# The even mixer of a two-layer trunk: v projected ahead of q and k, recurrence outputs ahead of attention outputs, slices of a quarter

## The chip, the cores and the metric

The kernel runs on one core of one Trainium2 chip. The metric is the device time of one execution in microseconds (us); less is better. PE is the engine of the matrix multiplications, DVE, ACT and POOL are the vector, scalar and GpSimd engines, and SP issues the loads of the weights.

## What is computed

A trunk of two layers runs over 256 rows of 1024 values. Each layer is a feed-forward block (FFN), a mixer, and another FFN; the mixer of layer 0 is "even", that of layer 1 is "odd" (retention). Only the even mixer matters here. It runs differential attention and a recurrence (RWKV-7) side by side behind one input projection and joins them in one output projection:

```python
def diff_rwkv_mixer(h, w_in, w_out, ...):
    z = h @ w_in
    za, zb = z[..., :A_COLS], z[..., A_COLS:]        # attention | recurrence
    qa, ka, va = jnp.split(za, 3, axis=-1)
    ...
    oa = diff_attention(qa, ka, va, lam)             # softmax 0 - lam * softmax 1, per head
    oa = rms_norm(oa, subln) * (1.0 - lam_init)
    ob, v_b = rwkv7_time_mix(zb, mu, vec, w_up, a_up, g_up, v_first, vres)
    mix = jnp.concatenate([oa, ob], axis=-1)
    return mix @ w_out, v_b

def rwkv7_time_mix(zb, ...):
    zs = token_shift(zb, mu)                         # z + (previous row - z) * mu
    r, k, v, xw, xa, xg = jnp.split(zs, B_SPLITS, axis=-1)
    ...
    y = rwkv7_recurrence(rh, heads(decay), kh, vh, kk, heads(a))
    y = head_group_norm(y, ln_w, ln_b)
    y = y + bonus                                    # sum(r*k*r_k) * v, per head
    return y * g, v
```

## The kernel before

The 256 rows are two blocks of 128 (b = 0 and 1). Every product is made of three multiplications of split operands: a weight chunk of 128x1024 lands as `raw`, ACT rounds it into `wh` (L307), DVE subtracts to get the rest `wl` (L308), and PE multiplies the high and low halves of the activations with them. These casts and splits run through the whole kernel, and each `wh` waits for a buffer that PE has finished reading.

The even mixer is one generator per block, `even(b, ...)`, and the loop `run` interleaves the two by the table `turns`, which is made from `EVEN_ORDER`. It is a list of seven pieces of the input projection: k, r and "low" (the low-rank inputs) and v feed the recurrence; q2, k2 and v2 feed the attention. The pieces are the stream: long runs of multiplications whose operands are there early. Between them go jobs with long chains over several engines: `feature` (shifted k and r, through a transposition on PE), `low_rank`, then `rwkv_features` (which ends in the multiplications `pn` that need `kk` from ACT and `fr` from POOL), `rwkv` (the core: doubling steps L1175 to L1183 that invert small triangular matrices, then the grams `pk`, the outputs `py` and the norm), and `attention`. A piece of the stream stops at a `yield "slice", 1.4` in `proj_slices` or `features_slices`, and there the loop may put in one step of a job; the numbers beside each `yield` are estimates of how long a step takes on PE and when its results are there. `spawn` gives each job a rank, and the lowest rank that is due goes first. `room` keeps a step back until one of two PSUM buffers for such steps should be free. PE then runs in exactly this order (`manual_schedule`); the other engines follow an order that the scheduler makes from it.

Inside a block the order is: k, r, low, q2, k2, v, v2. Block 0 projects q and k for both blocks. `value` (the recurrence's v) scales z on ACT, moves it down one row by a DMA on POOL's queue (`zs<-z`, and for block 1 the last row of block 0, `ups`), and mixes on DVE in three operations (L840 to L842). It takes its buffers from `t2`, a ring of five that also holds the `z`, `zm`, `kk`, `low`, `mu`, `lnw` and `lnb` of the other jobs. After v2 come the output projections: each of the four rows of weights takes one transposed input, `att0`, `att1` from the attention and `mr0`, `mr1` from the recurrence, which `turn` makes with two PE transpositions (L387), ACT (L391, L394) and DVE (L392, L395). Then `post` normalises and adds to x, and the next FFN begins with transpositions of x (L434).

The output of the recurrence is a chain on DVE: copy of `py` (ACT L1303), mean (L1313), subtraction (L1315), square (ACT L1316), variance (L1318), a power on POOL (L406), scaling (L1320 to L1322), and the gate (L1325).

Of the kernel before, what the change touches and what calls it, by code (L numbers as in the profile page):

```python
# [41 lines left out]
U_FFN, U_EVEN, U_ODD = 3 * NCH, 17, 32  # L42


EVEN_ORDER = ("k", "r", "low", "q2", "k2", "v", "v2")
PLAN = [("ffn", 0, 0), ("even", 0, 0), ("ffn", 0, 1), ("ffn", 1, 0), ("odd", 1, 0), ("ffn", 1, 1)]
SIZES = {"ffn": U_FFN, "even": U_EVEN, "odd": U_ODD}

# [57 lines left out]
def _layout(inputs):  # L106
    a = {n: np.asarray(v) for n, v in inputs.items()}
    f = np.float32

    def cols(w, k_tiles=4):  # L110

        k, n = w.shape
        return w.reshape(-1, k_tiles, P, n).transpose(0, 2, 1, 3).reshape(-1, P, k_tiles * n)

    def ffn(l, j, i):
        c0, c1 = JOINT.get(i, JOINT[None])
        w = a["ffn_wgu"][l, j]

        solo = w.reshape(2, 4, P, 2, NCH, 256).transpose(4, 0, 2, 1, 3, 5).reshape(NCH, 2, P, 2048)
        both = w.reshape(8, P, 2, NCH, 256).transpose(3, 2, 1, 0, 4).reshape(NCH, 2, P, 2048)  # L120
        gu = np.concatenate([solo[:c0], both[c0:c1], solo[c1:]])
        dn = cols(a["ffn_wd"][l, j], 2)
        out = []
        for c in range(NCH):
            out += [gu[c, 0], gu[c, 1]]
            if c:
                out.append(dn[c - 1])
        return out + [dn[NCH - 1]]

    def even():  # L130
        w, out = a["even_w_in"][0], []
        b0 = 1536
        at = {"k": b0 + 512, "r": b0, "v": b0 + 1024, "q2": 0, "k2": 512, "v2": 1024}
        for c in EVEN_ORDER:
            if c == "low":
                out += list(cols(w[:, b0 + 1536 :], 8))
            elif c in ("q2", "k2"):
                out += [cols(w[:, i : i + 256], 8)[0] for i in (at[c], at[c] + 256)]
            else:
                out += list(cols(w[:, at[c] : at[c] + 512]))  # L140
        return out + list(cols(a["even_w_out"][0], 2))

    def odd():
        w, out = a["odd_w_in"][0], []
        wo = list(cols(a["odd_w_out"][0], 2))

        def ch(c):
            return list(cols(w[:, c : c + 512]))

        def head(c):  # L150
            return list(cols(w[:, c : c + 256], 8))

        for h in range(4):
            out += ch(2048 + h * 512) + ch(4096 + h * 512)
            if h:
                out += wo[2 * h - 2 : 2 * h]
            else:
                for c in range(0, 1024, 512):
                    out += head(c) + head(c + 256) + head(c + 1024) + head(c + 1280)
        return out + wo[6:8]  # L160

    units = []
    for i, (kind, l, j) in enumerate(PLAN):
        units += ffn(l, j, i) if kind == "ffn" else even() if kind == "even" else odd()
    wts = np.ascontiguousarray(np.stack(units))

    par = np.zeros((P, PR_N), f)

    def put(name, v):
        s, e = PR[name]  # L170
        par[: v.shape[0], s:e] = v

    nm = a["norms"]
    put("gpre", nm[:, 0::2].reshape(6, 8, P).transpose(2, 0, 1).reshape(P, 48))
    mu = a["rwkv_mu"][0]
    put("mu_r", mu[0:512].reshape(4, P).T)
    put("mu_k", mu[512:1024].reshape(4, P).T)
    s, _ = PR["mu_s"]
    par[:64, s] = mu[1536:1600]
    par[:64, s + 1] = mu[1600:1664]  # L180
    par[:, s + 2] = mu[1664:1792]
    w0, a0, k_k, k_a, r_k, ln_w, ln_b = a["rwkv_vec"][0]
    put("k_k", k_k.reshape(4, P).T)
    put("k_a", k_a.reshape(4, P).T)
    s, _ = PR["r_k"]
    for t in range(4):
        for h in range(2):
            par[h * 64 : h * 64 + 64, s + 2 * t + h] = r_k[t * P + h * 64 : t * P + h * 64 + 64]
    put("sub", a["diff_subln"][0][:, None])
    rows = np.concatenate([nm[:, 1::2].reshape(-1), mu[1024:1536], ln_w, ln_b, a["diff_lam"][0].reshape(-1)])  # L190
    ups = np.zeros((P, 3, 512), f)
    ups[:64, 0] = a["rwkv_w_up"][0]
    ups[64, 0] = w0
    ups[:64, 1] = a["rwkv_a_up"][0]
    ups[64, 1] = a0
    ups[:, 2] = a["rwkv_g_up"][0]
    c0, ce, co = _constants()
    return {
        "x": np.ascontiguousarray(a["x"].reshape(SEQ, D)),
        "wts": wts,  # L200
        "rows": np.ascontiguousarray(rows),
        "ups": ups,
        "c0": np.concatenate([c0, par], 1),
        "ce": ce,
        "co": co,
    }
# [6 lines left out]
class Trunk:  # L213
# [103 lines left out]
    def proj_slices(self, ps, u, first, last, xT, width=512):  # L317
        w = self.split[u]
        xh, xl = xT
        n = 2048 // width  # L320
        k0 = 0 if first else 8 - n
        mm = self.nc.tensor.matmul
        for i in range(n):
            h, l = w[2 * i // n]
            c = slice(i % (n // 2) * width, (i % (n // 2) + 1) * width)
            kt = k0 + i
            mm(ps[:, :width], lhsT=xh[:, kt, :], rhs=h[:, c], start=first and i == 0, stop=False)  # L327
            mm(ps[:, :width], lhsT=xh[:, kt, :], rhs=l[:, c], start=False, stop=False)  # L328
            mm(ps[:, :width], lhsT=xl[:, kt, :], rhs=h[:, c], start=False, stop=last and i == n - 1)  # L329
            if i == n // 2 - 1:  # L330
                yield "slice", 1.4

    def outp(self, acc, u, hT, first, last):
        w = self.split[u]
# [10 lines left out]
    def features_slices(self, ps, u):  # L345

        w, xh, xl = self.split[u], self.xh, self.xl
        mm = self.nc.tensor.matmul
        for t in range(2):
            o = ps[:, t * 256 : t * 256 + 256]  # L350
            for kt in range(8):
                h, l = w[kt // 4]
                c = slice(kt % 4 * 256 + t * P, kt % 4 * 256 + t * P + P)
                mm(o, lhsT=h[:, c], rhs=xh[:, kt], start=kt == 0, stop=False)
                mm(o, lhsT=h[:, c], rhs=xl[:, kt], start=False, stop=False)
                mm(o, lhsT=l[:, c], rhs=xh[:, kt], start=False, stop=kt == 7)
                if kt == 3 or (kt == 7 and not t):
                    yield "slice", 1.4

    def proj_parts(self, u, t):  # L360

# [340 lines left out]
    def even(self, b, u, l, j):  # L702
# [57 lines left out]
        def feature(ps, name, mu, om_at):  # L760
            z = scaled(ps, T2("z"))
            yield 0, 1.3
            yield from self.room(2.6)
            tp = transposes(z, 4)

            d = mx.tile([P, 4, P], F32, tag=f"av{'kr'.index(name)}" if b else f"f{name}", name=f"f{name}")
# [105 lines left out]
        for c in EVEN_ORDER:  # L872
            if c in ("q2", "k2"):
                for i in range(2):
                    if b == 0:
                        ps = self.ps("mm")
                        yield from self.features_slices(ps, u)
                        (queries if c == "q2" else keys)(i, ps)
                        self.stream_took = 1.4
                    else:  # L880
                        self.stream_took = 0
                    u += 1
                    if i and c == "k2":
                        att = self.spawn(1 + 3 * b, self.attention(b, S[f"qT{b}"], kT, rs), 1.5)
                    yield
                continue
            ps = self.ps("mm")
            if c != "low":
                yield from self.proj_slices(ps, u, True, False, xT)
                self.stream_took = 1.4  # L890
                u += 1
                if rs is None:
                    rs = self.rstd(b)
# [3 lines left out]
                    self.spread(b, rs)  # L897
            else:
                yield from self.proj_slices(ps, u, True, True, xT, 256)
            self.stream_took = 1.4  # L900
            u += 1
            if c in jobs:
                job = self.spawn(2 * b, jobs[c](ps))
                if c == "low":
                    core = S[f"core{b}"] = job
            else:
                with self.tc.high_priority(LIFT):
                    (value if c == "v" else values)(ps)
# [6 lines left out]
            return S["core0"]["done"] if b else "through1" in S  # L915

        acc = None
        for i, job in enumerate((att, att, core, core)):
            while not job["done"] or self.now < job["at"] or (acc is None and not free()):
                yield "wait"  # L920
            if acc is None:
                acc = [self.ps(("mm", "ac1")[b]) for _ in range(2)]
            self.outp(acc, u, S.pop(f"{'mr' if i > 1 else 'att'}{b}{i % 2}"), i == 0, i == 3)
            self.stream_took = 2.8
            u += 1
            if i == 3:
# [48 lines left out]
    def attention(self, b, qT, kT, rs):  # L975
# [5 lines left out]
        nsl = CE["nsl"][0]  # L981
        ss = self.small(4, "ss4", 2)
        ma = self.hx(b).bitcast(F32).rearrange("p (a t) -> p a t", a=4)
        for h0 in range(0, 4, H):
            heads = range(h0, h0 + H)

# [27 lines left out]
            for i in range(H):  # L1014
# [2 lines left out]
                    out=s[:, 0, i], in0=s[:, 0, i], scalar=ri[:, 0, i : i + 1], in1=s[:, 1, i],  # L1017
                    op0=ALU.mult, op1=ALU.add,
                )
            yield 1.7, 8.0  # L1020
            while f"av{b}" not in S or "pT" in S:
                yield
            S["pT"] = True
# [21 lines left out]
            yield 0.9, 0  # L1045
        r4 = self.power(ss, EPS, 4, "r4")
        V.tensor_tensor(out=ma, in0=ma, in1=r4[:, :, None].to_broadcast([P, 4, P]), op=ALU.mult)
        yield 0, 5.0
        for i in range(2):
            yield from self.room(1.6)  # L1050
            S[f"att{b}{i}"] = self.turn(b, ma[:, 2 * i : 2 * i + 2], S["sub"])
# [326 lines left out]
    def run(self):  # L1378
# [26 lines left out]
                    lag = 1 + pos[0] // LAG0[0]  # L1405
            return ahead < lag

        sizes = {"low": 1, "out": 4}
        turns, at = [], next(at for at, kind in bounds.items() if kind == "even")
        for c in EVEN_ORDER + ("out",):  # L1410
            n = sizes.get(c, 2)
            turns += [0, 1] * 2 if c in ("q2", "k2") else [0] * n + [1] * n

# [74 lines left out]
```

## Time and profile before

| | us |
|---|---|
| median of three runs | 1195.79 |
| the three runs | 1194.28, 1195.79, 1196.98 |
| the profiled execution: its own time | 1200.61 |
| its span, first to last instruction | 1198.8 |
| outside the span | 1.8 |
| PE busy | 1152.4 (96%) |
| DVE busy | 744.8 (62%) |
| ACT busy | 626.2 (52%) |
| mean granted clock of PE | 0.986 |

The profiled execution is 4.8 us above the median of the runs, and 1.8 us of it lie outside the span. PE is the engine to read: the stretch of the even mixer begins near 202 us and its last output projection starts at 410.3 us; the first FFN lies before it, three FFNs and the odd mixer behind it.

### The profile page before, as it was taken

The numbers are of one execution on the slowest core, as the hardware profiler recorded it, in microseconds if no ns is written. First come the engines' busy times: TensorE is split into PE (matmuls) and PEld (weight loads), VectorE is DVE, ScalarE is ACT, GpSimd is POOL, SyncE is SP. The second block draws the span as 40 slices with busy tenths as digits, with TensorE's granted clock in tenths as the row PEclk, the third lists the DMA queues.
The fourth block names the chain that finished last, engine by engine and source line by source line (L and its number), as shares of the span: only waits on it lengthen the run. The fifth ranks groups of instructions, "written<-read, shape, count | busy, mean of one in ns | idle before, by whom it ended". The sixth has DMA issues, their size and how long they took to land.

```text
span 1198.8 us, 18578 instructions
## 1 busy us (share of the span) xinstructions
PE 1152.4 (96%) x7314; PEld 955.5 (80%) x7314; DVE 744.8 (62%) x1124; ACT 626.2 (52%) x1054; POOL 51.7 (4%) x79
## 2 busy tenths in 40 slices
PE   6999999999999799999999999999999999999997
PEld 5888887788778687888878888877877777888886
DVE  6665667667663656656676666675545557566664
ACT  7554456763242555555565555575434456555552
POOL 0000000012120100000010000010000001000000
PEclk9999999999999899999999999999999999999999
DMA  9766245432320346555646555556534554656551
GB/s 361 278 209 198 89 134 184 144 120 85 115 89 1 122 149 220 179 190 179 206 138 214 195 182 175 194 188 210 176 98 160 172 168 158 209 184 189 191 192 37
DMA packets 55657, 200.26 MB, mean 167 GB/s; under 512 B 6289, under 2 KB 6545, under 8 KB 55569
## 3 DMA queue, kind: packets, MB, share of 16 engines
q1 hardware_dynamic: 54576, 196.45, 49.2%
q0 software_dynamic: 704, 2.10, 0.6%
q8 instruction: 57, 0.93, 0.3%
q10 hardware_dynamic: 288, 0.52, 0.1%
q14 instruction: 32, 0.25, 0.1%
HBM read 197.47 MB, written 1.05 MB: 166 GB/s over the span
## 4 chain that ended last, share of the span: by engine, by line
PE 77%; DMA 8%; DVE 7%; ACT 4%; issue 2%; POOL 1%; SPq 0%; DVEq 0%; POOLq 0%; ACTq 0%
PE ps L370 22%; PE ps L371 11%; PE ps L341 7%; PE ps L343 7%; PE ps L342 7%; DMA raw<-in_wts_dram 7%; PE ps L327 5%; PE ps L329 4%; PE ps L328 4%; DVE wl L308 3%; ACT wh L307 2%; PE yp L619 1%; DMA x<-in_x_dram 1%; PE tp L387 1%; PE tp L434 1%
## 5 line engine op out<-in xcount | busy, mean ns | idle before, releaser
L308 DVE TENSOR_TENSOR wl<-raw,wh 128x1024 fp32r<-128x1024 f32 (+1 forms) x368 | 442.2, 1207 | 258.5 <-ACT wh L307 256.7
L307 ACT CAST wh<-raw 128x1024 fp32r<-128x1024 f32 (+1 forms) x368 | 379.9, 1038 | 240.6 <-PE ps L370 74.1
L370 PE MATMUL ps<-xp,wh 128*128 128x512 f32 x1312 | 467.4, 398 | 5.7 <-DVE gate L380 2.7
L371 PE MATMUL ps<-xp,wl 128*128 128x256 f32 x1312 | 367.7, 280 | 0.0
L370 PEld LDWEIGHTS ps<-xp,wh 128*128 128x128 f32 x1312 | 245.9, 187 | 71.4 <-DVE gate L380 11.5
L371 PEld LDWEIGHTS ps<-xp,wl 128*128 128x128 f32 x1312 | 247.8, 189 | 1.5
L341 PE MATMUL ps<-wh,hx 128*128 128x512 f32 x432 | 173.7, 402 | 0.1
L342 PE MATMUL ps<-wl,hx 128*128 128x512 f32 x432 | 172.2, 399 | 0.0
L343 PE MATMUL ps<-wh,hx 128*128 128x512 f32 x432 | 171.9, 398 | 0.0
L327 PE MATMUL ps<-wh,xp 128*128 128x512 f32 (+1 forms) x320 | 132.4, 416 | 2.0 <-ACT xp L439 1.9
L328 PE MATMUL ps<-wl,xp 128*128 128x512 f32 (+1 forms) x320 | 126.4, 396 | 0.2 <-DVE wl L308 0.2
L329 PE MATMUL ps<-wh,xp 128*128 128x512 f32 (+1 forms) x320 | 125.5, 394 | 1.0 <-DVE xp L440 0.9
L341 PEld LDWEIGHTS ps<-wh,hx 128*128 128x128 f32 x432 | 82.1, 190 | 19.6 <-ACT hx L394 0.5
L343 PEld LDWEIGHTS ps<-wh,hx 128*128 128x128 f32 x432 | 81.9, 190 | 19.8
L342 PEld LDWEIGHTS ps<-wl,hx 128*128 128x128 f32 x432 | 82.2, 190 | 17.6
L327 PEld LDWEIGHTS ps<-wh,xp 128*128 128x128 f32 x320 | 61.2, 191 | 19.6 <-ACT xp L439 5.9
L329 PEld LDWEIGHTS ps<-wh,xp 128*128 128x128 f32 x320 | 61.1, 191 | 16.3 <-DVE xp L440 3.1
L379 ACT COPY gate<-ps 128x256 f32<-128x256 f32 x74 | 27.2, 368 | 88.1 <-PE ps L371 88.1
L328 PEld LDWEIGHTS ps<-wl,xp 128*128 128x128 f32 x320 | 61.6, 192 | 12.9 <-issue 1.9
L380 DVE TENSOR_TENSOR gate<-ps,gate 128x256 f32<-128x256 f32 x74 | 31.1, 421 | 58.1 <-ACT gate L379 58.1
L379 ACT COPY h<-ps 128x256 f32<-128x256 f32 x74 | 27.2, 367 | 50.1 <-PE ps L371 50.0
L440 DVE SCALAR_TENSOR_TENSOR xp<-tp,c,xp 128x128 fp32r<-128x128 f32 x96 | 30.5, 347 | 15.7 <-ACT xp L439 14.7
(269 smaller groups left out, 947.3 us busy)
## 6 DMA issues: line engine op xcount, KB each, us to landing
raw<-in_wts_dram SPq DMA_DIRECT2D x362, 512.0 KB, 4.6
gpost<-in_rows_dram SPq DMA_DIRECT2D x6, 512.0 KB, 6.1
x<-in_x_dram SPq DMA_DIRECT2D x4, 256.0 KB, 6.8
ups<-in_ups_dram SPq DMA_DIRECT2D x1, 768.0 KB, 6.4
mu<-in_rows_dram POOLq DMA_DIRECT2D x2, 256.0 KB, 4.0
lnw<-in_rows_dram POOLq DMA_DIRECT2D x2, 256.0 KB, 4.9
lnb<-in_rows_dram POOLq DMA_DIRECT2D x2, 256.0 KB, 5.4
dec<-in_co_dram SPq DMA_DIRECT2D x1, 512.0 KB, 7.2
```

The lines of the kernel that those rows point to most:

```text
L307: nc.scalar.copy(out=h[:, c], in_=r[:, c])
L308: nc.vector.tensor_tensor(out=l[:, c], in0=r[:, c], in1=h[:, c].bitcast(F32), op=ALU.subtract)
L327: mm(ps[:, :width], lhsT=xh[:, kt, :], rhs=h[:, c], start=first and i == 0, stop=False)
L328: mm(ps[:, :width], lhsT=xh[:, kt, :], rhs=l[:, c], start=False, stop=False)
L329: mm(ps[:, :width], lhsT=xl[:, kt, :], rhs=h[:, c], start=False, stop=last and i == n - 1)
L341: mm(acc[n], lhsT=hh[:, t], rhs=wh[:, c], start=first and t == 0, stop=False)
L342: mm(acc[n], lhsT=hh[:, t], rhs=wl[:, c], start=False, stop=False)
L343: mm(acc[n], lhsT=hl[:, t], rhs=wh[:, c], start=False, stop=last and t == 1)
L370: mm(ps, lhsT=h[:, c], rhs=both, start=kt == 0, stop=False)
L371: mm(ps[:, :256], lhsT=l[:, c], rhs=both[:, :256], start=False, stop=kt == 7)
L379: self.nc.scalar.copy(out=o, in_=ps[:, 256:])
L380: self.nc.vector.tensor_tensor(out=o, in0=ps[:, :256], in1=o, op=ALU.add)
```

## The change

Five things change, all in the even mixer, and no product is added or left out.

1. `EVEN_ORDER` puts v ahead of q2 and k2, and v2 waits for the event `formed1` (the features of block 1 are made).
2. The output projection takes `mr0`, `mr1` first and `att0`, `att1` last, and the rows of the weights are stored in that order; `turns` has block 0's and block 1's recurrence outputs first, then both attention outputs.
3. `proj_slices` and `features_slices` stop at every quarter (0.7) and not at every half (1.4).
4. The attention of block 1 makes scores and softmax of both head pairs first, and the transpositions and the product with the values after them.
5. The ranks: both recurrences go ahead of both attentions. Of the delays, `feature` asks for a room of 3.6, and the attention's last turn waits 6.5.

```diff
-EVEN_ORDER = ("k", "r", "low", "q2", "k2", "v", "v2")
+EVEN_ORDER = ("k", "r", "low", "v", "q2", "k2", "v2")
...
-        return out + list(cols(a["even_w_out"][0], 2))
+        wo = list(cols(a["even_w_out"][0], 2))
+        return out + wo[2:] + wo[:2]
...
-            if i == n // 2 - 1:
-                yield "slice", 1.4
+            if i % (n // 4) == n // 4 - 1 and i < n - 1:
+                yield "slice", 0.7
...
-                if kt == 3 or (kt == 7 and not t):
-                    yield "slice", 1.4
+                if kt % 2 and (kt < 7 or not t):
+                    yield "slice", 0.7
...
-            yield from self.room(2.6)
+            yield from self.room(3.6)
...
-                        att = self.spawn(1 + 3 * b, self.attention(b, S[f"qT{b}"], kT, rs), 1.5)
+                        att = self.spawn(2 + b, self.attention(b, S[f"qT{b}"], kT, rs), 1.5)
                     yield
                 continue
+            while c == "v2" and "formed1" not in S:
+                yield "wait"
...
-                job = self.spawn(2 * b, jobs[c](ps))
+                job = self.spawn(b, jobs[c](ps))
...
-        for i, job in enumerate((att, att, core, core)):
+        for i, job in enumerate((core, core, att, att)):
...
-            self.outp(acc, u, S.pop(f"{'mr' if i > 1 else 'att'}{b}{i % 2}"), i == 0, i == 3)
+            self.outp(acc, u, S.pop(f"{'att' if i > 1 else 'mr'}{b}{i % 2}"), i == 0, i == 3)
...
+        probs = []
         for h0 in range(0, 4, H):
...
-            yield 1.7, 8.0
+            probs.append((heads, s))
+            yield 1.7, 0.5
+        yield 0, 7.5
+        for heads, s in probs:
+            h0 = heads[0]
             while f"av{b}" not in S or "pT" in S:
...
-        yield 0, 5.0
+        yield 0, 6.5
...
-        sizes = {"low": 1, "out": 4}
+        sizes = {"low": 1}
-        for c in EVEN_ORDER + ("out",):
+        for c in EVEN_ORDER + ("out", "out"):
```

Line numbers below L760 grow by one with the change, those behind the attention by eight.

The first place is where v and the features of block 0 meet, after the input pieces k, r and low. On POOL before, the memset and the multiplications `fr` come first and the loads and shifts of v later:

```order
L1151 MEMSET work 32x8x32
L1095 TENSOR_TENSOR fr<-fr,ta 128x256 x4
L1252 MEMSET work 128x512
L1205 COPY inv_2521<-work 32x8x32 x4
L1192 COPY work<-work 32x8x32
L1200 COPY work<-work 32x8x32
L271 DMA mu<-in_rows_dram 128x512
L833 DMA zs<-z 127x512
L838 DMA ups<-z 1x16x32
L271 DMA mu<-in_rows_dram 128x512
L833 DMA zs<-z 127x512
L835 DMA zs<-ups 1x16x32
```

On POOL of the change, the loads and shifts of both blocks' v (`mu`, `zs`, `ups`) stand ahead of the two `fr` of block 0:

```order
L272 DMA mu<-in_rows_dram 128x512
L834 DMA zs<-z 127x512
L839 DMA ups<-z 1x16x32
L1103 TENSOR_TENSOR fr<-fr,ta 128x256
L272 DMA mu<-in_rows_dram 128x512
L834 DMA zs<-z 127x512
L836 DMA zs<-ups 1x16x32
L1103 TENSOR_TENSOR fr<-fr,ta 128x256
```

What moved: the transfers of both blocks' v, which stood behind all four `fr`, now stand ahead of block 0's second one, three of them ahead of its first.

On ACT at the same place, before, the first square of `kk` (L1098) follows the features, the exponentials `w` and four query copies:

```order
L1088 ACTIVATE ta<-ta,om 128x128 x4
L1082 ACTIVATE kk<-fk,c_73 128x128
L860 ACTIVATE hx<-ps 128x128 x2
L1077 ACTIVATE w<-pc 128x258
L1078 ACTIVATE w<-pc 128x258
L860 ACTIVATE hx<-ps 128x128 x2
L1098 ACTIVATE kk<-kk 128x256
```

On ACT of the change, the second pair of `kk` copies (L1090) and its square (L1106) stand behind weight casts, and around the scaled `z` of block 1's v:

```order
L308 CAST wh<-raw 128x1024
L1085 ACTIVATE w<-pc 128x258
L1086 ACTIVATE w<-pc 128x258
L308 CAST wh<-raw 128x1024 x2
L1090 ACTIVATE kk<-fk,c_73 128x128 x2
L716 ACTIVATE z<-ps,rs_2007 128x512
L1096 ACTIVATE ta<-ta,om 128x128 x2
L1106 ACTIVATE kk<-kk 128x256
```

What moved: `kk` of the second half of block 0 is now made after two more casts and around v's `z`; its buffer is one of the five of `t2`.

The second place is DVE when the keys are made. In the change, the second half of `akT` (the attention's keys of two of the four heads, for both blocks) stands behind the whole output chain of block 0's recurrence:

```order
L406 TENSOR_SCALAR pw_in<-var 128x8
L1328 TENSOR_TENSOR work<-work,r_3720 128x512
L1329 TENSOR_TENSOR work<-work,lnw 128x512
L1235 TENSOR_TENSOR gram<-pm,ce 128x512
L1330 TENSOR_TENSOR work<-work 128x512
L1235 TENSOR_TENSOR gram<-pm,ce 128x512
L1333 TENSOR_TENSOR work<-pg,work 128x512
L850 TENSOR_TENSOR akT<-ps,rsb 128x512
L309 TENSOR_TENSOR wl<-raw,wh 128x1024
L1001 SCALAR_TENSOR_TENSOR s<-sp,rs_1922,ce 128x512 x2
```

Before, the same operation stands between the splits of the weights and a `kk` product, far ahead of every output chain:

```order
L1176 TENSOR_TENSOR work<-p_2773,ce 128x8x32
L308 TENSOR_TENSOR wl<-raw,wh 128x1024
L1182 TENSOR_TENSOR work<-p_2819,work 128x256
L849 TENSOR_TENSOR akT<-ps,rsb 128x512
L1183 STREAM_TRANSPOSE work<-work 128x256
L308 TENSOR_TENSOR wl<-raw,wh 128x1024
L1176 TENSOR_TENSOR work<-p_2886,ce 128x8x32
L997 SCALAR_TENSOR_TENSOR s<-sp,rs_1922,ce 128x512 x2
```

What moved: the keys' scaling went from ahead of the recurrence's outputs to right behind the first one's gate (L1333).

The third place is DVE at the last recurrence output, before:

```order
L1313 TENSOR_REDUCE mean<-work 128x8
L1314 TENSOR_SCALAR mean<-mean 128x8
L1315 TENSOR_TENSOR work<-work,mean 128x512
L1318 TENSOR_REDUCE var<-work 128x8
L405 TENSOR_SCALAR pw_in<-var 128x8
L405 TENSOR_SCALAR pw_in<-ss_2993 128x4
L1320 TENSOR_TENSOR work<-work,r_4212 128x512
L1047 TENSOR_TENSOR hx<-hx,r_4222 128x512
L1321 TENSOR_TENSOR work<-work,lnw 128x512
L1322 TENSOR_TENSOR work<-work 128x512
L395 SCALAR_TENSOR_TENSOR hx<-tp,sub,hx 128x256 x2
L1325 TENSOR_TENSOR work<-pg,work 128x512
```

And with the change, the same chain from its square on (L1326 is the variance, L1333 the gate, `hx` is the attention's output of block 0):

```order
L309 TENSOR_TENSOR wl<-raw,wh 128x1024
L1326 TENSOR_REDUCE var<-work 128x8
L309 TENSOR_TENSOR wl<-raw,wh 128x1024
L406 TENSOR_SCALAR pw_in<-var 128x8
L406 TENSOR_SCALAR pw_in<-ss_3809 128x4
L1328 TENSOR_TENSOR work<-work,r_4038 128x512
L1055 TENSOR_TENSOR hx<-hx,r_4062 128x512
L1329 TENSOR_TENSOR work<-work,lnw 128x512
L309 TENSOR_TENSOR wl<-raw,wh 128x1024
L1330 TENSOR_TENSOR work<-work 128x512
L396 SCALAR_TENSOR_TENSOR hx<-tp,sub,hx 128x256
L1333 TENSOR_TENSOR work<-pg,work 128x512
```

What moved: three splits `wl` of the output weights now stand inside the chain, where there was none.

## Rows read from the trace of the kernel before

**Rows 1.** Windows by stage: start:end, duration, busy us (count) of each engine, clock, DMA.

```profile
200.00:425.00 225.00, 202.60 (x2557) 171.66 (x2556) 141.85 (x302) 111.58 (x264) 31.74 (x43) 0.93 0.31 102
425.00:800.00 375.00, 372.25 (x1894) 309.73 (x1893) 243.26 (x325) 205.13 (x311) 3.67 (x6) 1.00 0.57 186
```

**Rows 2.** PE's waits from 200 to 425 us: total us, times, longest.

```profile
PE tp L387 <- DVE hx L1047: 6.4, 1, 6.4
...
PE tp L456 <- DVE rw L454: 2.1, 1, 2.1
PE p L1175 <- DVE work L1183: 1.9, 1, 1.9
...
PE pm L1232 <- DVE inv L1222: 1.3, 2, 0.9
PE tp L387 <- DVE mr L392: 1.2, 1, 1.2
PE pk L1293 <- ACT work L1303: 1.0, 2, 0.6
...
PE p L1181 <- DVE work L1176: 0.8, 1, 0.8
PE pa L817 <- ACT th L811: 0.7, 1, 0.7
PE op L1037 <- ACT pT L1031: 0.7, 1, 0.7
...
PE p L1189 <- DVE ri L1013: 0.3, 1, 0.3
```

**Rows 3.** Windows around gaps; the number behind the POOL column is PE's granted clock.

```profile
249.00:252.00 3.00, 3.00 (x28) 3.00 (x27) 1.46 (x6) 2.79 (x9) 0.00 (x0) 1.00 0.00 0
278.00:281.00 3.00, 3.00 (x58) 2.94 (x48) 0.42 (x1) 0.00 (x0) 0.29 (x1) 0.50 0.05 14
356.00:359.00 3.00, 3.00 (x11) 2.47 (x10) 1.26 (x2) 0.59 (x1) 0.00 (x0) 0.54 0.78 247
395.00:398.00 3.00, 2.86 (x9) 2.08 (x8) 2.36 (x5) 0.90 (x2) 0.00 (x0) 0.50 0.00 0
398.00:401.00 3.00, 3.00 (x10) 2.30 (x9) 0.00 (x0) 0.82 (x1) 0.00 (x0) 0.57 0.00 0
422.00:425.00 3.00, 3.00 (x11) 2.42 (x11) 0.81 (x3) 0.81 (x4) 0.00 (x0) 0.59 0.06 22
```

**Rows 4.** Timeline of POOL: start, us, operation, [idle before <- releaser].

```profile
258.50 2.87 POOL L1095 TENSOR_TENSOR fr<-fr,ta 128x256 f32<-128x256 f32 x1 [2.57 <-DVE ends L1097]
...
277.10 0.72 POOL L1095 TENSOR_TENSOR fr<-fr,ta 128x256 f32<-128x256 f32 x1 [1.44 <-DVE ends L1097]
...
298.17 0.57 POOL L833 DMA_DIRECT2D zs<-z  x1 [1.37 <-ACT z L715]
```

**Rows 5.** Groups of DVE, 202 to 411 us: busy us, mean ns, idle before.

```profile
L308 DVE TENSOR_TENSOR wl<-raw,wh 128x1024 fp32r<-128x1024 f32 x33 | 40.4, 1230 | 21.4 <-ACT wh L307 21.4
```

**Rows 6.** Timeline of PE at the end of core 1.

```profile
387.24 1.08 PE L1324 MATMUL pg<-ups,sxg 128*128 128x512 f32 x2
```

**Rows 7.** Timeline of DVE, core 1's output.

```profile
387.85 0.69 DVE L1313 TENSOR_REDUCE mean<-work 128x8 f32<-128x512 f32 x1 [2.21 <-ACT work L1303]
...
390.22 0.69 DVE L1318 TENSOR_REDUCE var<-work 128x8 f32<-128x512 f32 x1 [0.76 <-ACT work L1316]
...
396.74 0.68 DVE L1325 TENSOR_TENSOR work<-pg,work 128x512 f32<-128x512 f32 x1
```

**Rows 8.** Timeline of POOL in the tail.

```profile
391.20 2.64 POOL L406 TENSOR_TENSOR r<-pw_in,mhalf 128x8 f32<-128x8 f32 x2 [6.77 <-DVE pw_in L405]
```

**Rows 9.** Timeline of PE, two slices and a change of work.

```profile
284.47 0.39 PE L328 MATMUL ps<-wl,xp 128*128 128x512 f32 x1
284.70 0.39 PE L329 MATMUL ps<-wh,xp 128*128 128x512 f32 x1
285.04 0.74 PE L1175 MATMUL p<-work 32*32 32x32 f32 x64
```

More of the change, by code (lines that the diff above doesn't have):

```diff
@@ L878, in even @@
                         (queries if c == "q2" else keys)(i, ps)
-                        self.stream_took = 1.4
+                        self.stream_took = 0.7
                     else:
@@ L889, in even @@
                 yield from self.proj_slices(ps, u, True, False, xT)
-                self.stream_took = 1.4
+                self.stream_took = 0.7
                 u += 1
@@ L899, in even @@
                 yield from self.proj_slices(ps, u, True, True, xT, 256)
-            self.stream_took = 1.4
+            self.stream_took = 0.7
             u += 1
             if c in jobs:
-                job = self.spawn(2 * b, jobs[c](ps))
+                job = self.spawn(b, jobs[c](ps))
                 if c == "low":
```

## The prediction

> **What bounds the kernel now.** I read the windows by stage first [rows 1]. Behind 425 us PE is busy 372.25 of 375 us at a clock of 1.00: nothing that this change touches is to be gained there. In the 225 us of the even mixer it is busy 202.60, at 0.93. So the stake is 22.4 us of idle PE and what the lower clock costs. Next the list of PE's waits [rows 2]: one of 6.4 us (the turn of `hx` at the end waits for DVE), 2.1 at the seam to the FFN, 1.9, 0.8 and 1.0 in the recurrence, 1.3, 1.2 and 0.7 around the keys and the attention, 0.7 at `pa`. They are all waits of short steps for chains on DVE, ACT and POOL; there the order on PE decides.
>
> Last the clock, by windows [rows 3]. The one that follows the wait of 0.7 at `pa` reads 1.00; behind the wait of 1.9 it reads 0.50, behind 6.4 us 0.50 and 0.57 in two windows of 3 us, behind 2.1 us 0.59, and behind the pair of 1.2 and 1.3 at 355 us 0.54. 0.50 is the lower level of 1.2 GHz, 1.00 that of 2.4. A window of 3 us at 0.50 does half the work, so the drop costs 1.5 us after 1.9, 3·0.50·(2.86/3) + 3·0.43 = 2.7 after the long one, 1.2 at the seam and 1.4 at the keys. A longer wait than about 1 us therefore costs its length and some 1.5 us more.
>
> **What before pays, by place.** Front (features of block 0): 0.7. Recurrence: 1.9 + 0.8 + 1.0 and two waits of 0.3 [rows 2] are 4.3, with two drops (behind 1.9 and 0.8) 7.3. Keys and scores: 1.2 + 1.3 + 0.7 = 3.2, with 1.4 it is 4.6. Outputs: 6.4 + 2.7 = 9.1. Seam: 2.1 + 1.2 = 3.3. Together 25.0. The change takes the same work through another order, so I price each place anew.
>
> **Front: dearer.** v of block 1 is now projected directly ahead of `pn`, whose second half needs `kk` from ACT and `fr` from POOL. When PE ends v, ACT must still scale block 1's z, and POOL, which takes its queue in order, must issue `zs` and `ups` behind that z before it may multiply `fr`; DVE's product for `fr` stands behind the first half of `pn`. So from the end of v: z 0.7 (taken as long as the 128x512 operations of DVE shown further down), two issues of 0.57, and the multiplication, 0.7 to 2.9 [rows 4], of which I take 1.5, nearer to the shorter: 3.3 us, against 0.9 us of `pn` work. That is a wait of 2.4 (1.6 to 3.8). Then `px` waits for DVE's L1167, which stands behind a split of 1.23 [rows 5] and v's mixing; `pl`, `pw` and `pa` cover most of it, and I take 1.0 (0 to 1.5). The two waits follow one another like the pair in the tail, so the clock costs 2.7 (1.5 to 2.7). Sum 6.1, before 0.7: **+5.4**.
>
> Here a rule speaks against the change. The longer `fr` of [rows 4] ran while DVE was splitting weights, the shorter one beside little. The Trainium skill, page "SBUF — State Buffer", section "SBUF: two separate sides", says that DVE with two SBUF inputs and GpSimd share one port pair as an exclusive lock, so that the loser waits for the whole instruction. A split has two SBUF inputs and stands right behind DVE's product for `fr`. By the rule alone the multiplication would take 0.72 + 1.23 = 2.0, and the sum would be 0.5 us more; two splits in a row would give the 2.9 of the rival below.
>
> **Recurrence: cheaper.** `q2` and `k2` now lie between the doubling steps as slices of six multiplications, and the large wait of 1.9 has 12 of them in its place. Following the order, at six places PE still has less to do between L1183 and L1189 of a step than the product and the transposition on DVE take. None is longer than the 1.0 of two `pk` in [rows 2] nor shorter than 0.3: I take 0.6 each, 3.6, and one drop of 1.5. Sum 5.1, before 7.3: **−2.2** (−4.0 without a drop, 0 with two).
>
> **Keys and scores: nearly the same.** `pm` of block 1 stands behind an `inv` copy that DVE does after a split: 1.4 (1.23 and a little [rows 5]). The scores then need `akT`, which is behind the output chain of core 0 on DVE. That chain, from the last `py`, which `pg` follows at 387.24 [rows 6], to the gate's end at 397.42 [rows 7], took 10.2 us for core 1. For core 0 it has no second power (half of 2.64 [rows 8] less), but two grams of 0.7, a split of 1.23 and `akT` 0.7 more: 12.2. PE has 9.9 us to do meanwhile (an estimate: the slices between, at 0.23 us a multiplication of 512 and half that for 256 [rows 9], `pg`, the solves and the wait of 1.4). That leaves 2.3. With 0.5 for small ones and 0.8 for the clock it is 5.0, before 4.6: **+0.4** (−2.5 where the grams hide in the wait for the power, +1.5 where POOL is late).
>
> **Outputs: little gained.** Before, nothing stood behind the last recurrence but its chain, and PE idled 6.4 us. Now PE has `pg`, one product with the values, 18 multiplications of v2 and a first output projection of 12 behind the last `py`: 0.7 + 0.8 + 30·0.23, the transpositions of the second probabilities 0.5 and four changes of work, about 9.3 us. But DVE's chain has three splits inside, each behind its cast, and two operations of the softmax: 10.2 + 3·1.23 + 2·0.48, less the 0.76 that lay idle for the square [rows 7], is 14.1. Two waits, first for `hx`, then for the second output, share 14.1 − 9.3 − 0.3 = 4.5; casts behind the sums of squares on ACT add 0.5, so 5.0 (0.6 where all splits hide, 6.2 where none does). With a drop for two waits of 2.3 and 0.6 for the turns behind, 7.9; before 9.1: **−1.2**.
>
> **Seam: a little cheaper.** The last attention turn and x of the FFN have 24 and 9 output multiplications ahead of them now, so 2.1 becomes about 1.5 in pieces, with a drop of 1.2 it is 2.7: **−0.6** (−2 to +1).
>
> **Slices: a cost.** In the order PE changes work 14 times more in this stretch (231 groups of the same work, 217 before). A change costs 0.34 − 0.23 = 0.11 us [rows 9]: **+1.5**.
>
> **Nothing, and what hides it.** The stored order of the weights moves the same bytes. The ranks, the room of 3.6 and the lag of 6.5 make no instruction; they act through the order. Attention 1's scores ahead of its transpositions cost two buffers that are free there.
>
> Sum: +5.4 − 2.2 + 0.4 − 1.2 − 0.6 + 1.5 = **+3.3 us**. The profiled execution took 1200.61 (span 1198.8 and 1.8 around it), so its like would take 1203.9; that execution lies 4.8 above the median of the runs, and I forecast the median: 1195.79 + 3.3 = 1199.1.
>
> **Rivals.**
> *The outputs hide (other side).* The splits of the output weights run ahead of the second chain because their loads and buffers come early: DVE then does 10.2 us against 9.3 on PE. For it: the splits wait for casts, 21.4 us of DVE's idle time in this stretch [rows 5], and a cast that is early takes its split out of the chain. Against: each of the three `wh` waits for a buffer that PE frees only in the 18 multiplications of v2. Decides: the wait ahead of the second output is under 1 us. Then 5.0 + 2.3 become 0.6, −6.7: 1199.1 − 6.7 = 1192.4.
> *No change.* POOL's `fr` takes 0.7 as at 277.10 [rows 4], `px` is covered, and the front costs 1.6 + 1.5 and not 6.1: 3.3 − 3.0 = 0.3, 1196.1. For it: at that row DVE was also in the features.
> *Much dearer.* `fr` 2.9 by the row at 258.50 and by the port rule above, so +1.4 and px 1.5, +0.5; core 0's power late on POOL behind core 1's two 512-wide products, +1.5: 1202.5.
> *The change does nothing:* excluded, the order of all engines differs from 240 us on.
>
> **How the numbers follow.** Main case 0.39, its own range 1196.5 to 1201; outputs hide 0.24; no change 0.24; much dearer 0.13. The two sides together need 1192.4 and 1202.5 inside with the bounds of the terms: 1189.5 to 1205. Under 0.2% (2.4 us) a measurement of this kernel can hardly tell from nothing. Of the main case 0.27 lies above 1198.2 and 0.12 below; with the dearer one slower is 0.40. Faster: the rival with 0.24 and 0.05 of "no change", 0.29. Same: 0.31.
>
> **What would show it.** In the trace of after: a wait of `pn` for ACT or POOL of 1.6 to 3.8 us near 250 us with a clock of 0.50 behind; no wait over 1.2 in the doubling steps; the first scores waiting for `akT`; two waits of the turns, for `hx` and for the second output, of 5 us in all; no 6.4 us anywhere. I am wrong if `pn` waits under 1 us (then no change or faster), or if the splits of the output weights start before the last `py`.

## The result, and the profile after

The change makes the kernel slower: 1210.15 us (median of four, 1205.22 to 1212.98) against 1196.38 before; the ratio is 1.0112, 95% interval 1.0073 to 1.0152. The forecast was slower too, but by 3.3 us, and the time lies 5 us above the range of 1189.5 to 1205. The four times of the change spread over 8 us; those of before over 3.

The windows by stage of the profiled execution (its own time 1205.22) answer to [rows 1]:

```profile
200.00:430.00 230.00, 204.28 (x2544) 171.47 (x2543) 141.50 (x298) 109.71 (x259) 32.30 (x43) 0.93 0.31 99
430.00:800.00 370.00, 368.46 (x1883) 307.60 (x1882) 239.36 (x317) 201.07 (x301) 3.62 (x5) 1.00 0.56 186
```

Behind the mixer nothing changed. In it PE is idle 25.7 us of 230 (22.4 of 225 before), at the same mean clock of 0.93. The list of PE's waits answers to [rows 2] (total, times, longest):

```profile
PE tp L388 <- DVE work L1333: 3.0, 1, 3.0
PE p L1205 <- issue: 2.9, 1, 2.9
PE p L1189 <- issue: 2.3, 2, 1.2
...
PE tp L388 <- DVE hx L1055: 1.9, 1, 1.9
PE pm L1240 <- DVE inv L1230: 1.6, 2, 1.3
PE pn L1118 <- POOL fr L1103: 1.5, 1, 1.5
PE pn L1117 <- ACT kk L1106: 1.3, 1, 1.3
PE p L1189 <- DVE work L1184: 1.1, 2, 0.6
PE sp L998 <- DVE akT L850: 0.9, 1, 0.9
...
PE p L1197 <- issue: 0.9, 1, 0.9
...
PE tp L457 <- DVE rw L455: 0.7, 1, 0.7
```

The waits of 6.4, 1.9 and 2.1 are gone. The 1.3 and 1.5 of `pn`, and 1.9 + 3.0 at the outputs, have come, as forecast. But three rows say "issue": PE waited for nothing that the profile shows, 6.5 us in all with two small ones. No row of [rows 2] did. PE's timeline at the longest shows where (start, us, operation, [idle before <- releaser]):

```profile
300.25 0.59 PE L1205 MATMUL p<-work 32*32 32x32 f32 x26
303.76 0.22 PE L1205 MATMUL p<-work 32*32 32x32 f32 x2 [2.92 <-issue]
...
303.83 0.71 PE L1207 MATMUL p<-work 32*32 32x32 f32 x15
```

It stands still within a run of 32x32 multiplications, 2.92 us, between two of the same group. In these 4 us the transfers were (GB/s in 40 slices of 0.1 us, then the queue):

```profile
GB/s 287 369 369 328 410 246 164 246 0 123 164 123 123 164 41 0 0 0 0 0 0 0 0 0 0 0 0 0 0 0 0 0 0 0 0 0 0 0 0 0
...
q8 instruction: 1, 0.02, 1.5%
```

Behind 301.5 us no transfer starts any more. Among the last is one packet of the queue named "instruction": it starts at 301.35 and takes 0.96 us, and PE goes on at 303.76. DVE, ACT and POOL idle too from 301.4 us on. The same holds for each of the six stops of this trace: it ends 2.3 to 2.4 us behind the start of such a packet (276.94 behind 274.56, 293.63 behind 291.30, 297.56 behind 295.30).

The clock, in windows that answer to [rows 3] (the number behind the POOL column):

```profile
255.00:258.00 3.00, 3.00 (x18) 2.58 (x17) 3.00 (x8) 2.83 (x5) 0.00 (x0) 1.00 0.45 106
258.00:261.00 3.00, 0.49 (x3) 0.30 (x2) 3.00 (x9) 2.34 (x5) 2.56 (x4) 0.81 0.51 163
261.00:264.00 3.00, 2.71 (x39) 2.53 (x40) 1.70 (x5) 0.69 (x2) 0.48 (x2) 0.50 0.64 206
264.00:267.00 3.00, 3.00 (x9) 1.97 (x10) 2.32 (x6) 1.12 (x3) 0.00 (x0) 0.50 0.56 205
267.00:270.00 3.00, 2.88 (x72) 2.46 (x72) 2.60 (x5) 1.91 (x6) 1.70 (x3) 0.50 0.25 75
270.00:273.00 3.00, 3.00 (x19) 2.78 (x19) 1.95 (x6) 0.38 (x1) 0.00 (x0) 0.50 0.88 251
273.00:276.00 3.00, 2.84 (x128) 2.56 (x127) 1.42 (x4) 1.08 (x3) 0.00 (x0) 0.91 0.36 141
349.00:352.00 3.00, 3.00 (x11) 2.52 (x11) 1.80 (x3) 1.04 (x1) 1.13 (x1) 0.50 0.02 8
393.00:396.00 3.00, 3.00 (x9) 2.33 (x8) 0.12 (x1) 0.00 (x0) 0.00 (x0) 0.50 0.02 7
```

Behind the two waits of `pn` it is at 0.50, the lower level, until past 273 us, though PE is then busy 2.7 to 3.0 of every 3 us. That costs about 6 us (half of PE's busy time in the 13.6 us from 259.9 to 273.5); twice what the tail's stretch of [rows 3] cost. In the second profile, further down, it lasts 10 us and costs 5.

**The account.** From the first transposition of block 1's low inputs (243.8 us before, 242.6 after) to the start of the last output multiplication (410.3 and 420.0), from two profiles of each kernel, in us:

| | before | before, again | after | after, again |
|---|---|---|---|---|
| waits for other engines | 14.7 | 14.6 | 13.3 | 14.6 |
| standing still, "issue" | 0 | 1.0 | 6.5 | 6.0 |
| lost to the lower clock while busy (half of that time) | 9.6 | 10.4 | 13.6 | 14.7 |
| the rest: PE's work at full clock | 142.3 | 142.4 | 143.9 | 143.7 |
| sum | 166.5 | 168.4 | 177.4 | 178.9 |

The means differ by 10.7: 5.8 of standing still, 4.1 of clock, 1.5 of work, and 0.7 less in the waits. The stretch behind is 2.9 shorter, since PE waits 1.3 less at the seam and has no lower clock there (1.7 before), and the one ahead 0.9. The profiles thus show some 7 us of the 14, for before's two (1200.6 both) lie above its median.

The mean clock that each run lists fills the gap. On one chip 11 runs of before had 0.9891 over a span of 1195.8, six of the change 0.9817 over 1209.0. Span times (1 − clock) is 13.0 and 22.1 us: 9.1 of the 13.2 us lie in the clock (some of it idle time at the low level), 4.1 outside it. That share of the clock is probably an upper bound: over the 80 runs of before on four chips, one us more of it went with 0.65 us more of time.

### The profile page after: what moved, and what is told of

The parts are those of the page before. It is cut to its first block, busy times and chain, and to the rows that moved or that the text cites. A ratio compares the mean times of both kernels' runs of the same rounds, so it can differ in the third digit from the quotient of the medians.

```text
span 1203.5 us, 18600 instructions
## 1 busy us (share of the span) xinstructions
PE 1155.7 (96%) x7314; PEld 957.3 (80%) x7314; DVE 746.0 (62%) x1124; ACT 626.0 (52%) x1054; POOL 52.2 (4%) x79
## 4 chain that ended last, share of the span: by engine, by line
PE 79%; DVE 6%; DMA 5%; ACT 4%; issue 3%; POOL 1%; SPq 0%; DVEq 0%; POOLq 0%; ACTq 0%
PE ps L371 23%; PE ps L372 12%; PE ps L344 7%; PE ps L342 7%; PE ps L343 7%; DMA raw<-in_wts_dram 5%; PE ps L330 4%; PE ps L328 4%; PE ps L329 4%; DVE wl L309 3%; ACT wh L308 2%; PE ps L355 1%; PE yp L620 1%; PE tp L435 1%; PE tp L388 1%
## 5 line engine op out<-in xcount | busy, mean ns | idle before, releaser
L441 DVE SCALAR_TENSOR_TENSOR xp<-tp,c,xp 128x128 fp32r<-128x128 f32 x96 | 30.3, 346 | 14.4 <-ACT xp L440 13.2
```

## The experiments

Theory A is that PE runs out of instructions, theory B that the front's wait and its long stretch of lower clock are the loss. The rival of both is my sum, in which waits for other engines decide. The table gives for each the median's difference to before on the same chip, the interval of the ratio, and how the mean of all its runs splits, against before's runs: time lost to the clock (span times 1 − clock) and the rest.

| run | us over before | ratio, 95% | clock | rest |
|---|---|---|---|---|
| after_again | 14.4 | 1.0084 to 1.0136 | +9.1 | +4.1 |
| halves | 12.1 | 1.0073 to 1.0115 | +7.3 | +4.1 |
| v_back | 14.2 | 1.0091 to 1.0137 | +9.7 | +4.0 |
| out_only | 12.2 | 1.0066 to 1.0107 | +11.9 | −0.8 |
| probe_burst | 13.9 | 1.0101 to 1.0144 | +5.2 | +9.1 |
| probe_spread | 2.8 | 1.0004 to 1.0039 | −2.3 | +4.9 |
| pn_later | 5.3 | 1.0024 to 1.0059 | +3.8 | +0.9 |
| v_only | 10.9 | 1.0071 to 1.0121 | +7.5 | +3.1 |
| before_warm | 0.9 | 0.9975 to 1.0020 | −2.3 | +2.6 |
| after_warm | 9.3 | 1.0044 to 1.0092 | +2.9 | +5.9 |
| out_back | 18.8 | 1.0115 to 1.0182 | +12.7 | +6.3 |
| pn_mr | 6.6 | 1.0023 to 1.0068 | +5.6 | −0.2 |
| pn_later_halves | 25.0 | 1.0172 to 1.0221 | +14.9 | +8.7 |
| before_warm34 | 3.4 | 1.0003 to 1.0042 | −1.8 | +4.5 |

**after_again: the changed kernel once more.**

> The changed kernel once more, beside before on one chip. Its profile shows PE standing still for 6.5 us (1.10, 1.18, 0.92, 2.92 and two of 0.2) in the middle of runs of 32x32 multiplications, released by nothing that the trace shows; before has none. Theory A (PE is out of instructions there, because the change packs the small multiplications more densely than their instructions are loaded): it is there again, 4 to 12 us at the same lines, and the times spread over several us as they did. Theory B (the long half-clock stretch of 13 us behind the wait of pn is the loss, the standing still was a chance of one execution): no such idle time, the clock at 0.50 again from 260 to 273 us. Time by both 8 to 15 us over before.

The standing still is there again, 6.0 us, at nearly the same lines, and the lower clock behind `pn` too:

```profile
PE p L1189 <- issue: 4.0, 2, 2.5
...
PE p L1183 <- issue: 1.3, 1, 1.3
```

Both theories hold so far. The second profile of before (before_again) had 1.0 us of it, at one place (292.1 us), where the forecast said none, and a stretch at 0.50 from 245 to 256 us without any wait that is not in the first: before has both losses at times, and less of them.

> The kernel before, one more profile, so that the accounts do not hang on one execution of it. By all theories: no idle time that nothing releases, 14 to 16 us of waits for other engines and 7 to 11 us of lost clock in the mixer.

**probe_burst and probe_spread: the same 512 spare multiplications, in one run or apart.**

```diff
+    def burst(self, ps, n):          # n groups of 32 calls of 32x32, 64 multiplications in the trace
+        ...
+                    self.nc.tensor.matmul(o[Q[q], h], lhsT=self.ident[Q[q], Q[q]], rhs=self.ident[Q[q], Q[q]], ...)
+            if c == "v" and b == 0:  # burst
+                self.burst(ps, 8)
...
+            if c in "kr":            # spread: also ahead of q2 and k2
+                self.burst(ps, 1)
```

> Before with eight groups of 64 extra 32x32 multiplications in one run, ahead of block 0's v; their results are overwritten and nothing waits for them. By the mean of the groups in the trace (0.68 us each) they are 5.4 us of PE. Theory A (PE runs dry of instructions): the run takes more than 9 us, with idle time inside that nothing releases, each piece of it ending some 1 to 2 us behind a packet of the instruction queue; the kernel is 9 us or more slower. Theory B (a chance of one execution): the run takes 5.4 to 6 us without idle time, the kernel 3 to 6 us slower.

> Before with the same number of extra 32x32 multiplications, one group of 64 ahead of each of eight pieces of the projection (k, r of both blocks, q2, k2). Theory A: between two groups lie long multiplications, the instructions come in time: each group takes 0.7 us, no idle time without a releaser, the kernel 4 to 6 us slower. If bursts do not matter, the same time as with one run.

PE's timeline in the burst:

```profile
284.60 1.22 PE L266 MATMUL ps<-c 32*32 32x32 f32 x120
286.21 1.29 PE L266 MATMUL ps<-c 32*32 32x32 f32 x128 [0.39 <-issue]
290.21 1.93 PE L266 MATMUL ps<-c 32*32 32x32 f32 x128 [2.72 <-issue]
293.94 1.93 PE L266 MATMUL ps<-c 32*32 32x32 f32 x128 [1.79 <-issue]
297.40 0.33 PE L266 MATMUL ps<-c 32*32 32x32 f32 x8 [1.52 <-issue]
```

After the first 120 it stops every 128, with 6.4 us of idle time that nothing releases; the run takes 13.1 us, partly at the lower clock (mean 0.70), and the kernel is 13.9 slower. Here too each stop ends 2.2 to 2.7 us behind the start of a packet of the instruction queue. Spread, the groups take 0.75 us each and PE stops in none of them. It does stand still for 2.4 us just behind the last group, from 276 to 287 us, where before did not:

```profile
PE p L1192 <- issue: 1.6, 1, 1.6
...
PE ps L363 <- issue: 0.7, 1, 0.7
```

The kernel is 2.8 slower, less than the 5.4 us of work and than the 4 to 6 expected. The page counts 61 packets on the instruction queue in both, 57 before:

```profile
q8 instruction: 61, 1.00, 0.3%
```

Four packets more for 512 multiplications and 512 weight loads is one for 256 instructions, or 128 multiplications: the distance of the stops. The 7314 multiplications of before and as many weight loads are 57 times 256, too. Theory A is shown for a burst, and by the packets ahead of each stop for the standing still of the change. The Trainium skill, page "Runtime: NRT & Kernel Launch", section "Instruction fetch mechanics", says that PE's instructions come in blocks of 16 KiB, 256 instructions, and that the cost of crossing to the next is mostly hidden. The size agrees (0.93 MB in 57 packets). That it is mostly hidden doesn't hold for the burst, with 6.4 us idle; it held inside the groups that lay apart.

**halves: slices of a half again.** `yield "slice", 1.4` as before, the rest of the change kept.

> The change with slices of a half again (two stops to a piece, 1.4), all else kept. Theory A: with 12 and not 6 long multiplications between the small ones the instructions come in time: standing still falls under 1.5 us, and the time falls by 5 to 8 us to some 4 us over before. Theory B: the front keeps its wait and its clock; the time falls by the 1.5 us of the added changes of work only, to 10 us over before.

The standing still falls to 0.7 us, as theory A says. The time falls by only 2 us, by intervals that overlap:

```profile
PE tp L388 <- DVE work L1333: 7.2, 1, 7.2
PE pm L1240 <- DVE inv L1230: 4.9, 2, 4.6
```

Waits of 7.2 and 4.9 stand in its place (3.0 and 1.6 with quarters): what the quarters cost in standing still they save in waits, by finer placing.

**v_only and v_back: the list.** `EVEN_ORDER` alone changed in before, and alone put back in the change.

> Before with v ahead of q2 and k2 and nothing else of the change (slices of a half, outputs and ranks as before). My step for the front: pn waits 2 to 3 us for kk and fr and the clock is at 0.50 for over 6 us behind it, 4 to 8 us slower than before. Rival: with the ranks of before block 1's attention and the outputs are unchanged, so nothing is lost behind; then within 2 us of before. Theory A: with halves hardly any idle time without a releaser, under 1.5 us.

> The change with v behind q2 and k2 again (the list of before), all else kept, quarters too. Theory A: the small multiplications then lie between v's and v2's multiplications of 512 columns, twice as long as those of q2 and k2, so standing still falls under 2 us and the time by 5 us or more. Theory B: v is not ahead of pn, so its waits (2.8 us) and the long stretch at 0.50 go, 8 to 9 us less, to about before. Both can hold; idle time without a releaser and the clock of 260 to 275 us tell how much is whose.

v_only is 10.9 slower, more than forecast, and not where I said: `pn` doesn't wait at all; `py` waits for a gram (3.1) and `pk` for the state (2.0), and 6.4 at the end stay. So the list by itself costs three quarters of what the whole change does, without the wait that I priced. v_back is no faster than the change: with v behind, `pr` waits for it twice:

```profile
PE pr L1272 <- DVE rv L843: 9.4, 2, 4.8
```

The waits of `pn` go there, as theory B says, but 9.4 us of others come, and 3.5 us of standing still stay, where theory A said under 2. A part that is put back alone doesn't give back its share.

**out_only and out_back: the outputs' order.** `enumerate((core, core, att, att))`, the turns and the stored order alone, and these alone put back.

> Before with the outputs of the recurrence first and nothing else of the change (the turns for the outputs in two groups, the weights stored so). The prediction gave the outputs 1.2 us less: two waits of 5 us in place of 6.4, a shorter drop of the clock. Theory A and B expect no idle time without a releaser and no long half-clock stretch: 0 to 3 us faster than before. A rival: without the later attention the attention outputs are early anyway, and what ends last is the second recurrence, now needed at once: 3 to 6 us slower than before.

> The change with the attention's outputs first again and the weights stored so; all else kept. My sum gave the outputs 1.2 us in the change's favour, so this would be 1 to 3 us slower than the change. Rival, from the run with the outputs alone (12 us slower than before): the recurrence's outputs first cost by themselves, and this is 4 us or more faster than the change. Theory A sees the standing still among the small multiplications unchanged, 4 to 7 us.

Alone it costs 12.2 us, more than either forecast, and by the split of the runs all of it is clock: the 6.4 of the tail stays, a wait of 1.8 for the second output comes behind it and one of 2.5 for a gram ahead. Put back in the change it makes 18.8, 4 to 5 us more than the change, by intervals that overlap a little (from 1.0115, up to 1.0136). With the ranks and the list of the change the new order is thus probably worth having; by itself it is not, and there the sign of my step was wrong.

**pn_later, after_warm: the front.** A longer delay ahead of `pn`, or spare multiplications in its waits.

```diff
-        yield 0, 4.5
+        yield 0, 8.0                 # pn_later
...
+            if not b and g:          # after_warm: 11 of 256 columns ahead of each half of the second pn
+                self.warm(whole, 11)
```

> The change with a delay of 8.0 in place of 4.5 ahead of pn, so that PE's list has some thirty feature multiplications ahead of it; all else kept. Theory B: the waits of 1.3 and 1.5 us for kk and fr go, and with them the drop of the clock from 260 to 273 us: dependency waits 2.8 less, clock loss 4 to 6 us less, the kernel 5 us or more faster than the change. Theory A: the loss without a releaser stays or grows (the small multiplications are pushed closer together), the kernel gains 0 to 3 us.

> The change with 11 spare multiplications of 256 columns in each of the two waits of pn (1.3 us each); nothing reads them. Theory B: the waits stay, but PE is busy in them, the clock does not fall to 0.50 at 260 us, and the kernel is 4 to 6 us faster than the change. Rival: what made the later variant with pn 30 groups behind 8 us faster is the order that comes with it, not the clock: 0 to 2 us faster.

pn_later is 8 to 9 us faster than the change: the clock's loss falls from 22 to 17 us, the standing still to 0.5 in its profile. It still waits 4.0 us for core 0's turn and 4.2 in the doubling steps. after_warm changes nothing but what PE does while it waits, and is some 5 us faster; the windows are at 1.00 where the change had 0.50 up to 267 us, and the clock falls only behind, for a shorter time:

```profile
258.00:261.00 3.00, 3.00 (x25) 2.76 (x24) 3.00 (x12) 2.81 (x8) 1.31 (x3) 1.00 0.50 160
261.00:264.00 3.00, 2.91 (x51) 2.60 (x50) 2.91 (x3) 1.52 (x3) 1.74 (x3) 1.00 0.73 213
264.00:267.00 3.00, 2.08 (x14) 1.22 (x10) 2.70 (x8) 1.18 (x3) 0.86 (x2) 1.00 0.78 262
267.00:270.00 3.00, 2.83 (x76) 2.55 (x75) 2.65 (x6) 2.25 (x5) 0.85 (x2) 0.79 0.77 235
270.00:273.00 3.00, 3.00 (x77) 2.73 (x76) 1.76 (x6) 0.00 (x0) 0.00 (x0) 0.64 0.71 217
```

So the idle PE in these waits brings the low clock at 260 us, and theory B holds for 5 to 6 of the 9 us of clock by the split of the runs (9.1 with the change, 3.8 and 2.9 here). What the clock alone gives in time is less sure: in both profiles the standing still falls as well, to 0.5 and 1.6 us from 6.0 and 6.5, so neither run takes theory B's loss away by itself. The rest of after_warm is 1.8 higher than the change's; 22 spare multiplications of 0.119 us are 2.6 us (an estimate).

**pn_mr, pn_later_halves: what is left.** pn_later with `yield 0.9, 13.0` for core 0's turn (8.5 before), or with halves.

> The change with pn later (8.0) and the turn of core 0's output later (13.0 in place of 8.5), where the run with pn later still waited 4.0 us for it. If waits and the clock behind them add up, as in the account, this takes another 4 to 5 us off: 1197 to 1199 us, level with before or a little faster. Rival: the wait is only moved (to the scores or the last outputs): 0 to 1.5 us off, 1201 to 1203.

> The change with pn later (8.0) and slices of a half. Tells the two causes apart: with the front's wait gone, the quarters cost the 1.5 us of more changes of work and the rest of the standing still, so this is 1 to 3 us faster than pn later alone (1202.7), if those are costs. Rival, from the run with halves alone: the halves bring waits of 4 to 7 us for pm and the outputs, since the small steps cannot be placed as finely: 3 us or more slower than pn later alone.

pn_mr takes that wait from 4.0 to 1.2 but not the time (6.6 over before, 5.3 for pn_later): the rival was right, and in its place stand a wait of `pr` (2.2) and more loss by the clock. Its time outside the clock equals before's (−0.2). pn_later_halves is 25 us slower; waits of 6.8, 5.8 and 5.1 come, as the rival said of steps that can't be placed as finely. With the front mended the quarters pay.

**before_warm, before_warm34: spare work in the tail of before.** 46 or 34 multiplications of 256 columns ahead of the last `tp` that waits 6.4 us.

> Before with 46 spare multiplications of 256 columns (5.5 us at 0.119 each) put where PE waits 6.4 us for the first transposition of the last attention output; their results are not read. If the lost clock behind the wait is a cost of its own (2.7 us by my sum), the kernel is 2 to 3 us faster, with the clock at 1.00 behind the wait. Rival: the lower clock there costs nothing in the end, since what follows waits for other engines anyway: within 1 us of before.

> Before with 34 and not 46 spare multiplications (4.0 us) in the wait of 6.4 us ahead of the last attention output, so that they end ahead of what PE waits for; with 46 the clock still fell there, and small waits came behind. If the drop behind the wait costs time, 1 to 2.5 us faster than before; if the lower clock costs nothing there, the same.

Neither is faster: 0.9 and 3.4 us over. The clock's loss falls by about 2 us in both, and the rest grows by more. In their profiles small waits of 0.8 to 2.2 us come ahead of the last outputs and the clock falls there all the same. That a drop costs time by itself isn't shown here; after_warm speaks for it. Both profiles also have 1.6 and 1.9 us of standing still, which the first of before hadn't. No version beat before.

## Why the prediction was wrong

The direction was right, and the likeliest case; the size was 10 us short, for one term that wasn't in the sum and one that was mis-sized. It would have been shorter still without luck: for PE's waits on other engines the sum had 1.6 us more than before (18.3 against 16.7), and the profiles show 2.0 less in the mixer and the seam.

**A term left out.** "Recurrence: cheaper" counted what PE waits for on DVE. These waits came out below the estimate (1.1 us at the doubling steps against 3.6). But the change packs these steps closer: behind several lie six multiplications of 256 columns, 0.7 us, where before mostly had twelve or more, or six of 512. PE then needs instructions faster than they come, and stands still 6 us. [rows 2] could not show it; that a group of 64 small multiplications takes 0.7 us, as 6 of 256 columns do, could have. Before has one dense place too, from 290 to 295 us, and there its second profile stood still for 1.0.

**The front's clock, mis-sized.** "The two waits follow one another like the pair in the tail, so the clock costs 2.7": the waits were 1.34 + 1.46 = 2.8 for `pn` (2.4 forecast) and none for `px` (1.0), but the clock stayed low for 13.6 us in one profile and 10.3 in the other, 6 and 5 us in place of 2.7. The sum took the price of a drop from single windows, as some 1.5 us behind any wait of over about 1 us. That doesn't hold from one execution to the next. The pair of waits near 355 us, 1.18 and 0.92 (the 1.3 of [rows 2] is two waits together), has a drop behind it in one profile of before and none in the other; behind the wait of 2.1 at 244 us the low clock lasts 3.4 us in one and 10.2 in the other.

**`fr` and the shared port.** The forecast's estimate by the rule of the Trainium skill, page "SBUF — State Buffer", section "SBUF: two separate sides", was 2.0 us for `fr`. It took 1.13, and DVE's product beside it 0.95 where its like took 0.42:

```profile
260.11 1.13 POOL L1103 TENSOR_TENSOR fr<-fr,ta 128x256 f32<-128x256 f32 x1
```

```profile
259.09 0.42 DVE L1100 TENSOR_TENSOR ta<-ta,fk 128x256 f32<-128x256 f32 x1
259.43 1.22 DVE L309 TENSOR_TENSOR wl<-raw,wh 128x1024 fp32r<-128x1024 f32 x1
260.57 0.95 DVE L1101 TENSOR_TENSOR ka<-ta,w 128x256 f32<-128x256 f32 x1
```

The estimate counted the whole split, but the split had begun 0.68 us ahead of `fr`. What was left of it, 0.54, and 0.72 are 1.26; what was left of `fr` behind the start of the product, 0.67, and 0.42 are 1.09. Both measured times lie 0.13 to 0.14 below, so the trace nearly agrees with the lock. In [rows 4] the 2.87 us lay beside two splits, 258.42 to 260.76: 2.26 and 0.72 are 2.98.

**Right in mechanism.** Keys and scores: `pm` 1.6 (1.4 forecast), `akT` 0.9 and 2.5 in the two profiles (2.3). Outputs: 1.9 + 3.0 = 4.9 (5.0); the rival that they hide is refuted. Seam: 0.7 without a drop (2.7 with one), 2 us better. Slices: the work at full clock is 1.5 more (+1.5).

**Clock over all runs.** My places gave the clock nearly the same loss before and after (8.3 and about 8.5). The runs give 9.1 more. In after_warm and pn_later 5 to 6 of it go, with the front's drop and part of the standing still; in the change's first profile a drop follows the longest standing still (304 to 307 us). The rest stays open, and so does why the other orders lose so much clock (out_only above all, +11.9 with few new waits): how long a low stretch lasts differs between executions of one kernel, before's too.

## What to carry to other kernels

Count instructions as well as time: two or three groups of 64 tiny multiplications with little long work between them can stop the matrix engine for 1 to 3 us each, and such rows say "issue" in the list of waits. An idle matrix engine costs its wait, and often a stretch of low clock behind it: 2.7 us in the tail here, 5 to 6 at the front. Its length didn't follow from the wait's, so give such a drop a wide range, and read it in more than one profile. Judge a reordering by the runs' mean clock and the profile's account of waits, standing still, clock and work together, and don't expect one part's share to come back when that part alone is undone.

## What the runs showed of the hardware that was not expected

A packet on the instruction queue carries 256 instructions, and small multiplications use one up in 1.4 us (128 at 0.68 us for 64); in a burst PE then took 3.5 to 4.0 us for each 128. In the 16 traces that have them, each stop of PE that nothing releases ends 2.2 to 2.9 us behind the start of such a packet. 512 spare multiplications spread out cost 2.8 us where they are 5.4 us of work, with the clock's loss 2.3 us lower than before's, and 2.4 us of standing still in the profile. Executions of before had mean clocks from 0.982 to 0.993.
